# First modulation by single chunks of 128 channels, squares of x on PE, and groups of fours at other places of two projections and layer 1

## The chip, the cores and the metric

The kernel runs on one core of one Trainium2 chip. The metric is the time of one execution on the device, in microseconds; of several runs the median counts. The profile is that of one further execution, which the hardware profiler recorded.

## The reference

A latent stream x of 256 tokens and a context of 256 tokens, both of width 2048, go through two layers. Each layer first modulates the RMS norm of its input by shift and scale, which are products of a conditioning vector (SiLU of c, or of c_ctx for the context) with large matrices `ada_w`. Cut to what the change touches:

```
def _modulate(x, w, shift, scale):
    return _rmsnorm(x, w) * (1.0 + scale) + shift
...
sc, scc = silu(c), silu(c_ctx)
shift_x, scale_x, gate_x = split((sc @ ada_w[i] + ada_b[i])[:, None, :], 3)
shift_c, scale_c, gate_c = split(scc @ ada_w[i] + ada_b[i], 3)
hx = _modulate(x, norm_w[i], shift_x, scale_x)
hc = _modulate(ctx, norm_w[i], shift_c, scale_c)
...
# layer 0: p = hx @ w_in, cut into q, k, v, gates; retention and Fourier mixing; y @ w_out
# layer 1: bg, cg, xt, g = split(hx @ w_in, 4); y = bg * conv3(cg * xt) * silu(g); y @ w_out
x = x + gate_x * y
```

At the end stands a last RMS norm. All numbers are float32.

## The kernel before

**Numbers in two parts.** Float32 products are made on PE (TensorE) from two parts of each number. `whi` is a weight rounded to PE's fast 32-bit type (ACT casts, L94), `wlo` is the rest (DVE subtracts, L59). Activations are stored as 256 tokens of high part beside 256 of low part. A matmul with `whi` as the stationary operand streams all 512 columns, one with `wlo` only the 256 columns of the high part.

**Groups and pieces.** `group_t` makes 256 output channels. It loads 1 MB of weights at a time (`raw`), splits it into four pieces of 512 columns, and issues for each piece eight matmuls: four with `whi` (H0 to H3) and four with `wlo` (L0 to L3). Their order is a table: LOW alternates L0 H0 L1 H1, HIGH alternates H0 L0 H1 L1, FOURS has the four H and then the four L. An argument `orders` gives a pair, the table of a group's first piece and that of all others; default is LOW for both. SETTLE is (HIGH, FOURS), AFTER is (HIGH, LOW). `project` (first projection `w0o`, last projection `w1o`) uses groups of 16 pieces, b = 0 to 6: SETTLE in b = 1, AFTER in b = 2. Layer 1 (`w1`) has for each b = 0 to 15 four groups of 8 pieces, in the order tcg, txt, tbg, tg; SETTLE stands in tcg, AFTER in txt, for b = 1 and 2.

**The start.** x arrives in four tiles `xT`. `norm_sums` squares them on ACT, adds them on DVE (`nacc`) and sums over the 128 partitions by two matmuls with `ones`; root and reciprocal give `rs_x`. The modulation of 256 channels (one e of eight) needs 4 MB of `ada0`, in four loads (`load_ada`); `gemv` multiplies each with the conditioning (tile `gemv` in the profile), `gather` copies the sums (`gs`), `modulation` adds their four strips by four small products with `cols` and makes scale and shift (`md`), `mod_stream` writes the modulated x (`hx`) or context (`hc`). Then `main_k` and `main_v` multiply these 256 channels with 1 MB of `w0s`, into k, q and v of the first two heads (`pk`, `pq`, `pvx`; for the context `pk`, `pvc`). The loop over e does the main matmuls of e beside the gemv of e + 2.

**What sets the order.** Each engine runs its instructions in order. The order is made by a scheduler at build time, which moves instructions past each other as its own timeline sees fit; the source gives the priorities. Loads go out on the queue of SP, in order, and wait for a free buffer: three for `raw`, one each for the two others that `load_ada` uses (L237 to L248). `bg` and `hook` put other work between the pieces: the later modulation vectors (`adaT`, DVE) and, in layer 0, retention and Fourier steps. The Fourier products of the last channel groups (`pP`, `py`, `pz`) stand between the pieces of the first projection's b = 0 and 1.

Of the kernel before, what the change touches and what calls it, by code (L numbers as in the profile page):

```python
# [20 lines left out]
D = 2048  # L21
# [3 lines left out]
P = 128  # L25
# [10 lines left out]
def body(tc, a, out):  # L36
    nc = tc.nc
    es = ExitStack()
    with es:
# [88 lines left out]
        HIGH = "H0 L0 H1 L1 H2 L2 H3 L3".split()  # L128
        FOURS = "H0 H1 H2 H3 L0 L1 L2 L3".split()

        SETTLE, AFTER = (HIGH, FOURS), (HIGH, LOW)

        def group_t(wd, i0, nkt, streams, orders=(LOW, LOW)):

            ps = [psum("gT") for _ in streams]
            last = nkt * 8 - 1
            for kt in range(nkt):
                raw = load_raw(wd[i0 + kt])
                bg()
                for pc, (hi, lo) in enumerate(split_w(raw)):  # L140
                    todo = orders[kt + pc > 0]
                    seen = set()
                    for what, j in ((x[0], int(x[1])) for x in todo):
                        k2, m = j // 2, j % 2
                        kc, c0 = kt * 8 + pc * 2 + k2, j * 128
# [104 lines left out]
        def norm_sums(tiles, rs, ps):  # L250
            acc = rp.tile([P, 4, 256], F32, tag="m4", bufs=2, name="nacc")
            for q in range(4):
                if q == 0:
                    nc.scalar.square(acc[:], tiles[q][:])
# [7 lines left out]
            nc.scalar.activation(rs[:], ps[:, 0:256], AF.Sqrt, bias=eps[:], scale=1.0 / D)  # L262
            nc.vector.reciprocal(rs[:], rs[:])

        scol = const.tile([P, 32], F32, name="scol")
        nc.scalar.activation(scol[:], cols[:, C_C:C_C + 32], AF.Silu)
        nc.vector.tensor_copy(sc32[:, :, 0:16], scol[:, 0:16].unsqueeze(2).to_broadcast([P, 16, 16]))
# [6 lines left out]
        load_x(xT, a["xT"])  # L274
        
        pk, pvx, pvc = psum("pk"), psum("pvx"), psum("pvc")
        norm_sums(xT, rs_x, pvx[:, 0, :])
        gp, pq = bank("gemv"), bank("pq")

        def gemv(raw, kq):  # L280
# [29 lines left out]
        def main_k(e, k2, w):  # L310
            hi, lo = w
            kc = 2 * e + k2
            for x, blocks in ((hx[e], kq_x), (hc[e], k_c)):
# [7 lines left out]
        def main_v(e, k2, w):  # L321
            hi, lo = w
            kc = 2 * e + k2
            for x, t in ((hx[e], pvx), (hc[e], pvc)):
# [14 lines left out]
            return (rp.tile([P, 512], F32R, tag="sga", bufs=2, name="whi"),  # L339
                    rp.tile([P, 512], F32R, tag="ot", bufs=2, name="wlo"))  # L340

        mds = [prepare(0, load_ada(0))]
        mod_stream(0, mds[0], 0)
        wraw = load_raw(a["w0s"][0])
        load_x(cT, a["ctxT"])
        norm_sums(cT, rs_c, pvc[:, 0, :])
        mod_stream(0, mds[0], 1)
        mds.append(prepare(1, load_ada(1)))
        mod_stream(1, mds[1], 0)
        mod_stream(1, mds[1], 1)  # L350
        wn = split_w(wraw, spare)
        for e in range(8):
            w = wn
            more = e < 6
            if e < 7:
                wraw = load_raw(a["w0s"][e + 1])
            raws = load_ada(e + 2) if more else None
            main_k(e, 0, w[0])
            if more:
                gemv(raws[0], 0)  # L360
            main_v(e, 0, w[1])
# [5 lines left out]
            main_k(e, 1, w[2])  # L367
            if more:
                gemv(raws[3], 3)
                gs = gather()  # L370
            main_v(e, 1, w[3])
# [455 lines left out]
        def project(wd, xs, gcol, xin, acc, first=None, post=None):  # L827


            def res(b, m, v, src):  # L830
                nc.vector.scalar_tensor_tensor(x1[b][:, m, :], v, mods[:, gcol + 2 * b + m:gcol + 2 * b + m + 1],
                                               src[:, m, :], op0=ALU.mult, op1=ALU.add)

            tot = None
            for b in range(8):
                src = xin(b)
                quiet[0] = b >= 7 - (post is not None)
                if b < 7:
                    t = first if b == 0 and first is not None else group_t(wd, 4 * b, 4, [xs], *({1: (SETTLE,), 2: (AFTER,)}.get(b, ())))[0]
                    s = lr(l1, t)  # L840
                    for m in range(2):
                        res(b, m, s[:, m, :], src)
                    if b == 0:
                        nc.scalar.square(acc[:], x1[b][:])
                    else:
                        sq = l1.tile([P, 2, 256], F32, tag="t2", bufs=5, name="sq")
                        nc.scalar.square(sq[:], x1[b][:])
                        add(acc[:], acc[:], sq[:])
                    for m in range(2 if post is not None else 0):
                        nc.scalar.activation(x1[b][:, m, :], x1[b][:, m, :], AF.Copy,  # L850
                                             scale=cols[:, post + 2 * b + m:post + 2 * b + m + 1])
                else:
                    t = group_d(wd, 4 * b, 4, xs)
                    tot = bank("tot")
                    for m in range(2):
                        mm(tot[:, 0:256], ones[:], acc[:, m, :], m == 0, False)

                    warm = l1.tile([P, 1], F32, tag="warm", name="warm")
                    nc.scalar.activation(warm[:], acc[:, 0, 0:1], AF.Sqrt)
                    sq = l1.tile([P, 2, 256], F32, tag="t2", bufs=5, name="sq")  # L860
                    for m in range(2):
                        res(b, m, t[:, m * 256:m * 256 + 256], src)
                        nc.scalar.square(sq[:, m, :], x1[b][:, m, :])
                        mm(tot[:, 0:256], ones[:], sq[:, m, :], False, m == 1)
            return rstd_bc(l1, tot[:, 0:256], D)
# [17 lines left out]
        w1 = a["w1"]  # L883
        y1 = []
        for b in range(16):
            tcg, = group_t(w1, b * 8, 2, [h1], *((SETTLE,) if b in (1, 2) else ()))
            scg = lr(l1, tcg, "scg", 2)
            txt, = group_t(w1, b * 8 + 2, 2, [h1], *((AFTER,) if b in (1, 2) else ()))
            z = lr(l1, txt, "z", 2)
            mul(z[:], z[:], scg[:])  # L890
            cv = l1.tile([P, 2, 256], F32, tag="cv", bufs=2, name="cv")
            for m in range(2):
# [47 lines left out]
def _layout(i):  # L940
# [19 lines left out]
    a["ada0"] = s.reshape(32, P, 2048)  # L960
# [72 lines left out]
```

## Time and profile before

| | |
|---|---|
| runs of the kernel | 1822.88, 1823.37, 1826.58 us; median 1823.37 |
| the profiled execution | 1826.86 us |
| its span, first to last instruction | 1825.1 us |
| mean granted PE clock | 0.988 |
| busy share of the span | PE 97%, DVE 68%, ACT 49% |
| from HBM | 397.03 MB, 219 GB/s over the span |

The span runs from the first instruction to the last; the execution's own time has 1.8 us around it. A row of a timeline gives start, duration, engine, line, operation and operands, and in brackets how long the engine was idle before it and what released it. A matmul's duration is longer than the distance to the next matmul's start, since they overlap. A float32 product that isn't in two parts (gemv, ones, cols) has two records in the trace.

The stages, by the timeline: modulation and first heads to about 142 us, layer 0 with retention and Fourier to about 740, first projection to 916, layer 1 from 920 to about 1630, last projection to the end.

### The profile page before, as it was taken

How to read it: one execution, taken by the hardware profiler on the slowest of the kernel's cores; microseconds unless marked ns; L12 is line 12 of the kernel's file. 1: busy time of each engine (PE TensorE's matmuls, PEld its weight loads, DVE VectorE, ACT ScalarE, POOL GpSimd, SP SyncE). 2: the span in 40 equal slices, each digit the busy share in tenths (PEclk: the TensorE clock that was granted, in tenths of full speed). 3: DMA queues.
4: the chain of work that ended last, by engine and by line, in shares of the span. 5: the costliest groups of instructions: out<-in, count | busy, mean ns of one | idle time of the engine just before them, and what ended most of it. 6: DMA issues, size and time to landing. Idle time of an engine off the chain costs nothing.

```text
span 1825.1 us, 25950 instructions
## 1 busy us (share of the span) xinstructions
PE 1777.8 (97%) x10086; PEld 1514.6 (83%) x10086; DVE 1248.0 (68%) x2001; ACT 901.9 (49%) x1493; POOL 0.2 (0%) x4
## 2 busy tenths in 40 slices
PE   5999999999989999999999999999999999999997
PEld 3667888888877888888978888888888888888887
DVE  5348858758469788777677888666666666665554
ACT  4225626345455455444555555555555555555553
POOL 0000000000000000000000000000000000000000
PEclk9999999999989899999999999999999999999999
DMA  9886656655435556577647777555555555555552
GB/s 388 341 315 259 233 212 221 240 207 208 166 117 217 199 188 216 194 295 295 231 155 264 296 277 281 197 191 185 187 196 195 185 185 191 197 189 185 187 193 105
DMA packets 58732, 400.82 MB, mean 220 GB/s; under 512 B 6512, under 2 KB 6896, under 8 KB 11376
## 3 DMA queue, kind: packets, MB, share of 16 engines
q1 hardware_dynamic: 58608, 399.16, 59.8%
q8 instruction: 79, 1.29, 0.3%
q14 instruction: 45, 0.37, 0.1%
HBM read 397.03 MB, written 2.10 MB: 219 GB/s over the span
## 4 chain that ended last, share of the span: by engine, by line
PE 94%; DVE 3%; DMA 1%; ACT 1%; issue 0%; SPq 0%; DVEq 0%; ACTq 0%
PE gT L56 71%; PE gN L56 7%; PE gD L56 3%; PE pu L56 2%; PE gemv L56 2%; PE o L56 2%; PE pk L56 1%; PE pvx L56 1%; PE pvc L56 1%; PE pd L56 1%; DMA raw<-ada 1%; PE S L56 1%; PE pq L56 1%; DVE wlo L59 1%; PE pP L56 1%; PE py L56 0%
## 5 line engine op out<-in xcount | busy, mean ns | idle before, releaser
L94 ACT CAST whi<-raw 128x512 fp32r<-128x512 f32 x1024 | 628.3, 620 | 627.3 <-PE gT L56 469.4
L59 DVE TENSOR_TENSOR wlo<-raw,whi 128x512 fp32r<-128x512 f32 x1024 | 693.2, 688 | 344.4 <-ACT whi L94 334.5
L56 PE MATMUL gT<-h,whi 128*128 128x512 f32 x2048 | 707.6, 394 | 0.7 <-DVE h L215 0.7
L56 PE MATMUL gT<-h,wlo 128*128 128x256 f32 x2048 | 560.8, 278 | 3.4 <-ACT h L214 3.4
L56 PEld LDWEIGHTS gT<-h,whi 128*128 128x128 f32 x2048 | 383.3, 188 | 89.0 <-DVE h L215 1.2
L56 PEld LDWEIGHTS gT<-h,wlo 128*128 128x128 f32 x2048 | 383.4, 188 | 5.6 <-ACT h L214 3.8
L56 PE MATMUL gT<-hx,whi 128*128 128x512 f32 x576 | 209.4, 398 | 0.0
L388 DVE CUSTOM_DVE_ANT_0 raw<-raw,scb 128x2048 f32<-128x2048 f32 x64 | 146.5, 2290 | 54.0 <-DMA raw<-adaT 50.8
L56 PE MATMUL gT<-hx,wlo 128*128 128x256 f32 x576 | 165.2, 287 | 2.8 <-ACT v L507 1.6
L56 PE MATMUL gT<-y,whi 128*128 128x512 f32 x448 | 150.9, 394 | 0.0
L56 PEld LDWEIGHTS gT<-hx,whi 128*128 128x128 f32 x576 | 108.8, 189 | 21.3
L56 PEld LDWEIGHTS gT<-hx,wlo 128*128 128x128 f32 x576 | 109.5, 190 | 10.0 <-DVE wlo L59 2.7
L56 PE MATMUL gT<-y,wlo 128*128 128x256 f32 x448 | 116.9, 278 | 0.0
L56 PEld LDWEIGHTS gT<-y,whi 128*128 128x128 f32 x448 | 82.9, 188 | 18.2
L198 ACT COPY lr_r<-gT 128x512 f32<-128x512 f32 x103 | 60.5, 587 | 65.7 <-PE gT L56 65.4
L56 PEld LDWEIGHTS gT<-y,wlo 128*128 128x128 f32 x448 | 82.1, 188 | 1.4
L56 PE MATMUL gT<-yA,whi 128*128 128x512 f32 x224 | 77.5, 398 | 0.0
L56 PE MATMUL gT<-yB,whi 128*128 128x512 f32 x224 | 76.9, 398 | 0.0
L65 DVE TENSOR_TENSOR t<-gT,lr_r 128x512 f32<-128x512 f32 x68 | 46.9, 689 | 29.9 <-ACT lr_r L198 29.7
L56 PE MATMUL gT<-yA,wlo 128*128 128x256 f32 x224 | 59.9, 281 | 0.6 <-DVE wlo L59 0.6
L56 PE MATMUL gN<-whi,hx 128*128 128x512 f32 x192 | 59.7, 392 | 0.0
L56 PE MATMUL gN<-whi,hc 128*128 128x512 f32 x192 | 59.7, 391 | 0.0
(283 smaller groups left out, 2162.0 us busy)
## 6 DMA issues: line engine op xcount, KB each, us to landing
raw<-w SPq DMA_DIRECT2D x168, 1024.0 KB, 4.8
raw<-adaT SPq DMA_DIRECT2D x64, 1024.0 KB, 4.9
raw<-ada SPq DMA_DIRECT2D x32, 1024.0 KB, 7.1
raw<-w0o SPq DMA_DIRECT2D x32, 1024.0 KB, 4.8
raw<-w1o SPq DMA_DIRECT2D x32, 1024.0 KB, 4.8
raw<-w0g SPq DMA_DIRECT2D x16, 1024.0 KB, 4.8
raw<-w0u SPq DMA_DIRECT2D x16, 1024.0 KB, 4.9
raw<-w0s SPq DMA_DIRECT2D x8, 1024.0 KB, 5.6
```

The source lines that it names most:

```text
L56: nc.tensor.matmul(o, l, r, start=start, stop=stop, skip_group_check=True)
L59: nc.vector.tensor_tensor(o, x, hi.bitcast(F32), op=ALU.subtract)
L65: nc.vector.tensor_tensor(o, x, y, op=ALU.add)
L94: nc.scalar.copy(hi, x)
L198: nc.scalar.copy(r[:], t[:, :, 256:512])
L388: nc.vector.tensor_tensor_reduce(out=raw[:], in0=raw[:], in1=scb[:], scale=1.0, scalar=0.0, op0=ALU.mult, op1=ALU.add, accum_out=gv[:, j:j ...
```

## The change

1. **Start.** The first 256 channels (e = 0) are modulated in two chunks of 128. The first four loads of `ada0` are laid out anew on the host, so that two loads hold all that one chunk needs. `load_first`, `first` and `mod_first` do load, gemv and modulation of one chunk; the main matmuls of x for a chunk follow it at once, those of the context stay in the loop (argument `only`). The loads of the second chunk go into other buffers than raw.
2. **Squares of x.** `norm_sums_pe` squares half a tile on ACT and sums it by two matmuls with ones, 16 in all; DVE adds nothing. The context keeps `norm_sums`.
3. **Fours.** SETTLE and AFTER are now lists of eight orders, one for each piece; `group_t` steps through the list it is given and begins again at its end. In `project`, b = 3 and b = 4 have SETTLE + AFTER (first half, second half of a group); b = 1 and 2 are LOW. In layer 1, tcg and txt keep theirs in b = 1 and 2, and tbg and tg get SETTLE and AFTER in b = 0 and 1, so that the two alternate from b = 0's third group to b = 2's second.

```diff
-        SETTLE, AFTER = (HIGH, FOURS), (HIGH, LOW)
+        SETTLE, AFTER = [HIGH] + [FOURS] * 7, [HIGH] + [LOW] * 7
...
-                    todo = orders[kt + pc > 0]
+                    todo = orders[(kt * 4 + pc) % len(orders)]
...
+        def norm_sums_pe(tiles, rs, ps):
+            for q in range(4):
+                for h in range(2):
+                    sq = rp.tile([P, 2, 256], F32, tag="t2", bufs=5, name="sq2")
+                    nc.scalar.square(sq[:], tiles[q][:, 2 * h:2 * h + 2, :])
+                    for k in range(2):
+                        i = 4 * q + 2 * h + k
+                        mm(ps[:, 0:256], ones[:], sq[:, k, :], i == 0, i == 15)
...
-        mds = [prepare(0, load_ada(0))]
-        mod_stream(0, mds[0], 0)
+        r0 = load_first(0)
         wraw = load_raw(a["w0s"][0])
+        r1 = load_first(1)
+        m0 = first(0, r0)
+        mod_first(0, m0, 0)
+        wn = split_w(wraw, spare)
         load_x(cT, a["ctxT"])
+        main_k(0, 0, wn[0], (0,))
+        main_v(0, 0, wn[1], (0,))
+        m1 = first(1, r1)
+        mod_first(1, m1, 0)
+        main_k(0, 1, wn[2], (0,))
+        main_v(0, 1, wn[3], (0,))
+        raws1 = load_ada(1)
         norm_sums(cT, rs_c, pvc[:, 0, :])
-        mod_stream(0, mds[0], 1)
-        mds.append(prepare(1, load_ada(1)))
+        mod_first(0, m0, 1)
+        mod_first(1, m1, 1)
+        mds = [None, prepare(1, raws1)]
...
-            main_k(e, 0, w[0])
+            streams = (0, 1) if e else (1,)
+            main_k(e, 0, w[0], streams)
...
-                    t = first if b == 0 and first is not None else group_t(wd, 4 * b, 4, [xs], *({1: (SETTLE,), 2: (AFTER,)}.get(b, ())))[0]
+                    t = first if b == 0 and first is not None else group_t(wd, 4 * b, 4, [xs], SETTLE + AFTER if b in (3, 4) else (LOW,))[0]
...
-            tcg, = group_t(w1, b * 8, 2, [h1], *((SETTLE,) if b in (1, 2) else ()))
+            tcg, = group_t(w1, b * 8, 2, [h1], SETTLE if b in (1, 2) else (LOW,))
...
-            tbg, = group_t(w1, b * 8 + 4, 2, [h1])
+            tbg, = group_t(w1, b * 8 + 4, 2, [h1], SETTLE if b in (0, 1) else (LOW,))
...
-            tg, = group_t(w1, b * 8 + 6, 2, [h1])
+            tg, = group_t(w1, b * 8 + 6, 2, [h1], AFTER if b in (0, 1) else (LOW,))
```

The new functions of the first chunk:

```
def first(k2, raws):
    for i in range(2):
        for j in range(8):
            t = j % 4
            mm(gp[32 * t:32 * t + 32, 0:256], sc32[:, i * 8 + j, :], raws[i][:, j * 256:j * 256 + 256],
               i == 0 and j < 4, i == 1 and j > 3)
    gs = rp.tile([P, 512], F32, tag="cst", name="gs")
    nc.vector.tensor_copy(gs[:, 0:256], gp[:, 0:256])
    for n in range(2):
        mm(gp[:, 2 * n:2 * n + 2], gs[:, n * 128:n * 128 + 128], cols[:, C_SEL:C_SEL + 2], True, True)
    ...
    return md
def mod_first(k2, md, s):
    dst, src, rs = ((hx, xT, rs_x), (hc, cT, rs_c))[s]
    modulate(rp, dst[0][:, k2, :], src[0][:, k2, :], md[:, 0, s:s + 1], md[:, 1, s:s + 1], rs)
```

**The order of the loads on SP.** Before, the queue at the start stands so (ada is a quarter of one e, xT and cT the tiles of x and of the context):

```order
L85 DMA raw<-ada 128x2048
L244 DMA raw<-ada 128x2048
L85 DMA raw<-ada 128x2048
L244 DMA raw<-ada 128x2048
L85 DMA raw<-w0s 128x2048
L235 DMA cT_103<-ctxT 128x1024
L235 DMA cT_104<-ctxT 128x1024
L235 DMA cT_105<-ctxT 128x1024
L235 DMA cT_106<-ctxT 128x1024
```

Now, on the same queue behind the same four tiles of x:

```order
L85 DMA raw<-ada 128x2048 x2
L85 DMA raw<-w0s 128x2048
L361 DMA raw<-ada 128x2048 x2
L235 DMA cT_103<-ctxT 128x1024
L235 DMA cT_104<-ctxT 128x1024
L235 DMA cT_105<-ctxT 128x1024
L235 DMA cT_106<-ctxT 128x1024
L85 DMA raw<-ada 128x2048 x2
L85 DMA raw<-w0s 128x2048
L244 DMA raw<-ada 128x2048 x2
```

The first w0s stands ahead of the second pair of ada. Of the four loads of e = 1, which came one after the other ahead of the second w0s, two come behind it now.

**PE around the second gemv.** Before, on PE, where the gemv of e = 1 and the first context matmuls meet (hx_80 and hc_88 are x and context of e = 0):

```order
L56 MATMUL gemv<-raw,sc_79 32x512 x8
L56 MATMUL pvc<-nacc,ones 128x256 x2
L56 MATMUL pk<-hx_80,whi 128x256 x2
L56 MATMUL pk<-hx_80,wlo 128x256
L56 MATMUL pk<-hx_80,whi 128x256 x2
L56 MATMUL pk<-hx_80,wlo 128x256
L56 MATMUL gemv<-raw,sc_79 32x512 x4
L56 MATMUL pk<-hc_88,whi 128x256
L56 MATMUL pvc<-whi,hc_88 128x512
L56 MATMUL gemv<-raw,sc_79 32x512 x4
```

Now, at the same place:

```order
L56 MATMUL pvx<-wlo,hx_80 128x512
L56 MATMUL pvc<-nacc,ones 128x256 x2
L56 MATMUL gemv<-raw,sc_79 32x512 x12
L56 MATMUL pk<-hc_88,whi 128x256
L56 MATMUL pvc<-whi,hc_88 128x512
L56 MATMUL pk<-hc_88,whi 128x256
L56 MATMUL pk<-hc_88,wlo 128x256
```

The matmuls of x for e = 0 are all ahead of this place; three quarters of the gemv stand in one piece ahead of all context matmuls. On ACT and DVE the cast and split of the second w0s has moved ahead of the root and the reciprocal of `rs_c`.

**PE in the first projection.** Before, part of b = 1 (py and pz are Fourier products):

```order
L56 MATMUL gT<-yA_2404,whi 128x512 x4
L56 MATMUL gT<-yA_2404,wlo 128x256 x2
L56 MATMUL py<-ph,zh 128x256
L56 MATMUL py<-ph,zl 128x256
L56 MATMUL gT<-yA_2404,wlo 128x256 x2
L56 MATMUL py<-pl,zh 128x256
```

Now, where b = 3 begins:

```order
L56 MATMUL gT<-yA_1550,whi 128x512
L56 MATMUL gT<-yA_1550,wlo 128x256
L56 MATMUL gT<-yA_1554,whi 128x512 x4
L56 MATMUL gT<-yA_1554,wlo 128x256 x4
L56 MATMUL gT<-yA_2444,whi 128x512 x4
L56 MATMUL gT<-yA_2444,wlo 128x256 x4
L56 MATMUL gT<-yA_2448,whi 128x512 x4
```

The fours stood among Fourier products and stand now among matmuls of the projection alone.

More of the change, by code (lines that the diff above doesn't have):

```diff
@@ L129, in body, with group_t @@
         FOURS = "H0 H1 H2 H3 L0 L1 L2 L3".split()
-        SETTLE, AFTER = (HIGH, FOURS), (HIGH, LOW)
-        def group_t(wd, i0, nkt, streams, orders=(LOW, LOW)):
+        SETTLE, AFTER = [HIGH] + [FOURS] * 7, [HIGH] + [LOW] * 7
+        def group_t(wd, i0, nkt, streams, orders=(LOW,)):
             ps = [psum("gT") for _ in streams]
@@ L263, in norm_sums @@
             nc.vector.reciprocal(rs[:], rs[:])
+        def norm_sums_pe(tiles, rs, ps):
[6 more added lines that the diff above has]
+                        mm(ps[:, 0:256], ones[:], sq[:, k, :], i == 0, i == 15)
+            nc.scalar.activation(rs[:], ps[:, 0:256], AF.Sqrt, bias=eps[:], scale=1.0 / D)
+            nc.vector.reciprocal(rs[:], rs[:])
         scol = const.tile([P, 32], F32, name="scol")
@@ L276, in body @@
         pk, pvx, pvc = psum("pk"), psum("pvx"), psum("pvc")
-        norm_sums(xT, rs_x, pvx[:, 0, :])
+        norm_sums_pe(xT, rs_x, pvx[:, 0, :])
         gp, pq = bank("gemv"), bank("pq")
@@ L308, in mod_stream, with main_k @@
                          md[:, 2 + k2, s:s + 1], rs)
-        def main_k(e, k2, w):
+        def main_k(e, k2, w, only=(0, 1)):
             hi, lo = w
             kc = 2 * e + k2
-            for x, blocks in ((hx[e], kq_x), (hc[e], k_c)):
+            for x, blocks in [((hx[e], kq_x), (hc[e], k_c))[i] for i in only]:
                 xh, xl = x[:, k2, 0:256], x[:, k2, 256:512]
@@ L319, in main_k, with main_v @@
                     mm(o, lo[:, c0:c0 + 128], xh, False, kc == 15)
-        def main_v(e, k2, w):
+        def main_v(e, k2, w, only=(0, 1)):
             hi, lo = w
             kc = 2 * e + k2
-            for x, t in ((hx[e], pvx), (hc[e], pvc)):
+            for x, t in [((hx[e], pvx), (hc[e], pvc))[i] for i in only]:
                 for m in range(2):
@@ L340, in spare, with load_first @@
                     rp.tile([P, 512], F32R, tag="ot", bufs=2, name="wlo"))
-        mds = [prepare(0, load_ada(0))]
-        mod_stream(0, mds[0], 0)
+        def load_first(k2):
+            got = []
+            for i in range(2):
+                if k2:
+                    raw = (rp.tile([P, 2048], F32, tag="v", bufs=1, name="raw") if i == 0
+                           else wp.tile([P, 2048], F32, tag="scb", bufs=1, name="raw"))
+                    nc.sync.dma_start(raw[:], a["ada0"][2 * k2 + i])
+                else:
+                    raw = load_raw(a["ada0"][2 * k2 + i])
+                got.append(raw)
+            return got
@@ new lines, in first @@
+        def first(k2, raws):
+            for i in range(2):
+                for j in range(8):
+                    t = j % 4
+                    mm(gp[32 * t:32 * t + 32, 0:256], sc32[:, i * 8 + j, :], raws[i][:, j * 256:j * 256 + 256],
+                       i == 0 and j < 4, i == 1 and j > 3)
+            gs = rp.tile([P, 512], F32, tag="cst", name="gs")
+            nc.vector.tensor_copy(gs[:, 0:256], gp[:, 0:256])
+            for n in range(2):
+                mm(gp[:, 2 * n:2 * n + 2], gs[:, n * 128:n * 128 + 128], cols[:, C_SEL:C_SEL + 2], True, True)
+            md = rp.tile([P, 4, 2], F32, tag="md", bufs=2, name="md")
+            for n in range(2):
+                c = C_AB0 + 16 * n + k2
+                add(md[:, n, :], gp[:, 2 * n:2 * n + 2], cols[:, c:c + 1].to_broadcast([P, 2]))
+            mul(md[:, 0, :], md[:, 0, :], cols[:, C_NW0 + k2:C_NW0 + k2 + 1].to_broadcast([P, 2]))
+            return md
@@ L344, in body @@
+        def mod_first(k2, md, s):
+            dst, src, rs = ((hx, xT, rs_x), (hc, cT, rs_c))[s]
+            modulate(rp, dst[0][:, k2, :], src[0][:, k2, :], md[:, 0, s:s + 1], md[:, 1, s:s + 1], rs)
+        r0 = load_first(0)
         wraw = load_raw(a["w0s"][0])
+        r1 = load_first(1)
+        m0 = first(0, r0)
+        mod_first(0, m0, 0)
+        wn = split_w(wraw, spare)
         load_x(cT, a["ctxT"])
+        main_k(0, 0, wn[0], (0,))
+        main_v(0, 0, wn[1], (0,))
+        m1 = first(1, r1)
@@ L346, in body @@
+        mod_first(1, m1, 0)
+        main_k(0, 1, wn[2], (0,))
+        main_v(0, 1, wn[3], (0,))
+        raws1 = load_ada(1)
         norm_sums(cT, rs_c, pvc[:, 0, :])
-        mod_stream(0, mds[0], 1)
-        mds.append(prepare(1, load_ada(1)))
+        mod_first(0, m0, 1)
+        mod_first(1, m1, 1)
+        mds = [None, prepare(1, raws1)]
         mod_stream(1, mds[1], 0)
         mod_stream(1, mds[1], 1)
-        wn = split_w(wraw, spare)
         for e in range(8):
@@ L357, in body @@
             raws = load_ada(e + 2) if more else None
-            main_k(e, 0, w[0])
+            streams = (0, 1) if e else (1,)
+            main_k(e, 0, w[0], streams)
             if more:
                 gemv(raws[0], 0)
-            main_v(e, 0, w[1])
+            main_v(e, 0, w[1], streams)
             if e < 7:
@@ L366, in body @@
                 gemv(raws[2], 2)
-            main_k(e, 1, w[2])
+            main_k(e, 1, w[2], streams)
             if more:
@@ L370, in body @@
                 gs = gather()
-            main_v(e, 1, w[3])
+            main_v(e, 1, w[3], streams)
             if more:
@@ L885, in body @@
         for b in range(16):
-            tcg, = group_t(w1, b * 8, 2, [h1], *((SETTLE,) if b in (1, 2) else ()))
+            tcg, = group_t(w1, b * 8, 2, [h1], SETTLE if b in (1, 2) else (LOW,))
             scg = lr(l1, tcg, "scg", 2)
-            txt, = group_t(w1, b * 8 + 2, 2, [h1], *((AFTER,) if b in (1, 2) else ()))
+            txt, = group_t(w1, b * 8 + 2, 2, [h1], AFTER if b in (1, 2) else (LOW,))
             z = lr(l1, txt, "z", 2)
@@ L959, in _layout @@
     s = s.reshape(2, 4, 4, P, 8, 256).transpose(4, 1, 3, 2, 0, 5)
-    a["ada0"] = s.reshape(32, P, 2048)
+    s = s.reshape(32, P, 2048)
+    f0 = np.stack([ada[0][:, D:D + 256], ada[0][:, 0:256]]).reshape(2, 2, 8, P, 2, P)
+    s[0:4] = f0.transpose(4, 1, 3, 2, 0, 5).reshape(4, P, 2048)
+    a["ada0"] = s
     g = np.concatenate([ada[0][:, 2 * D:].T, ada[1][:, D:2 * D].T, ada[1][:, 0:D].T, ada[1][:, 2 * D:].T])
```

## Prediction

> **What bounds the kernel now.** I read the page first, then windows of the first microseconds, the timeline of PE, DVE and ACT up to 50 us, and last the starts of single matmuls, since the change is mostly one of order on PE.
>
> ```profile
> PE 94%; DVE 3%; DMA 1%; ACT 1%; issue 0%; SPq 0%; DVEq 0%; ACTq 0%
> ```
> PE carries 94% of the chain that ended last. So time can come from two places alone: the start, where PE idles, and the pace of back-to-back matmuls. Both are touched.
>
> ```profile
> 0.00:20.00 20.00, 6.16 (x28) 1.93 (x28) 7.07 (x12) 8.99 (x10) 0.20 (x4) 1.00 0.90 349
> 20.00:40.00 20.00, 14.22 (x78) 8.83 (x74) 12.04 (x20) 7.63 (x12) 0.00 (x0) 0.83 1.02 419
> 40.00:60.00 20.00, 19.60 (x131) 13.54 (x131) 8.58 (x20) 6.92 (x14) 0.00 (x0) 1.00 0.91 367
> ```
> The second number of a row is PE's busy time, the last ones are the granted clock, the DMA share and GB/s. In the first 40 us PE idles for 19.6 us while the DMAs are full (419 GB/s in the second row). From 40 us on PE is full and the DMAs are not. So the start waits for data, not for PE.
>
> **The start, step by step.** When do loads land?
>
> ```profile
> 13.36 1.94 PE L56 MATMUL gemv<-raw,sc 128*32 128x512 f32 x8 [13.36 <-DMA raw<-ada]
> 20.72 1.07 PE L56 MATMUL gemv<-raw,sc 128*32 128x512 f32 x8 [0.50 <-DMA raw<-ada]
> 23.20 2.17 ACT L94 CAST whi<-raw 128x512 fp32r<-128x512 f32 x4 [4.84 <-DMA raw<-w0s]
> 25.84 0.58 PE L56 MATMUL pq<-hx,whi 128*128 128x256 f32 x1 [2.19 <-ACT hx L214]
> 41.82 2.18 ACT L94 CAST whi<-raw 128x512 fp32r<-128x512 f32 x4 [1.07 <-DMA raw<-w0s]
> ```
> The first and the fourth 1 MB load of ada land at 13.36 and 20.72: three loads in 7.36 us, 2.45 us per MB. The next, w0s, lands at 23.20, again 2.48 us later. The queue is thus a line of loads at about 2.47 us each, and the new SP order says when each lands: ada 13.4 and 15.8, w0s 18.3, the second pair of ada 20.7 and 23.2, ctxT (2 MB) by 28.2, then two quarters of the next ada at 30.7 and 33.2, **the second w0s at 35.7**, and the other two quarters at 38.1 and **40.6**. Before, all four quarters came ahead of that w0s (41.82), so the last of them by about 38.3: it moves back by some 2.4 us.
>
> ```profile
> 5.06 1.06 ACT L254 ACTIVATE nacc<-xT 128x1024 f32<-128x1024 f32 x1 [0.30 <-DMA xT<-xT]
> 15.78 2.08 PE L56 MATMUL pvx<-nacc,ones 128*128 128x256 f32 x4 [0.48 <-DVE nacc L65]
> 35.85 1.13 PE L56 MATMUL pvc<-nacc,ones 128*128 128x256 f32 x4
> 37.53 1.75 DVE L263 RECIPROCAL rs_c<-rs_c 128x256 f32<-128x256 f32 x1 [2.76 <-ACT rs_c L262]
> 40.40 0.39 PE L56 MATMUL pk<-hc,whi 128*128 128x256 f32 x1 [1.71 <-ACT hc L214]
> 40.95 1.06 PE L56 MATMUL gemv<-raw,sc 128*32 128x512 f32 x8
> 41.94 0.38 PE L56 MATMUL pk<-hc,whi 128*128 128x256 f32 x1
> 43.80 0.40 PE L56 MATMUL pk<-hx,whi 128*128 128x256 f32 x2
> 45.94 0.95 PE L56 MATMUL gemv<-cols,gs 128*128 128x2 f32 x8
> 48.62 0.39 PE L56 MATMUL pk<-hx,whi 128*128 128x256 f32 x1
> ```
> Squares of x on PE: 16 matmuls with ones in place of 2. Two cost 2.08 us at 15.78 and 1.13 us at 35.85, so 16 take 9 to 17 us. They start after the first half square (x is there at 5.06), at about 5.7, and run where PE idled; they end near 17.5, as the two did before (15.78 + 2.08 = 17.86). rs_x therefore comes no earlier. If they ran cold to the end (5.7 + 16.6 = 22.3) the first modulation would lose what it gains, and nothing later.
>
> First chunk: its two loads are there at 15.8, so its gemv follows the squares, near 17.5 to 19.7, and rs_x (0.47 us on ACT, 1.75 on DVE, both behind the squares) at 20.3. From the old end of gemv (20.72 + 1.07 = 21.79) to the first main matmul (25.84) were 4.05 us; without the wait, with half the copy, some 2.6 remain: **first main matmul near 22.9, 2.9 us earlier**.
>
> Is that kept? Not if the second round (e = 1) starts as before. It needs the last quarter of ada. The new PE order puts the gemv of quarters two to four in one piece ahead of the context's matmuls, and the sums that gather the modulation (cols) behind them. So: last quarter lands at 40.6, gemv 1.06, 41.7. Beside it the context's path: the second w0s is cast and split on ACT and DVE ahead of rs_c now (35.7 + 2.2 on ACT, lo done by 39.1), then the reciprocal 1.75 (40.9), then 1.12 to the first context matmul as before (37.53 + 1.75 = 39.28 to 40.40): 42.0. The context's matmuls: 10 of a chunk's 12 took 43.80 - 41.94 = 1.86, so 2.2 per chunk, 4.4 for both: 46.4. The four cols products 0.95: 47.4. From there to the first matmul of e = 1 were 48.62 - 46.89 = 1.73: **49.1 against 48.62, +0.5 us**. The early work was done while PE would have waited anyway. From there PE is full (19.6 of 20 us), so these 0.5 us run through to the end. Bounds: -2.9 (all of the earlier start kept) and +2.9:
>
> ```profile
> 22.30:25.70 3.40, 1.05 (x8) 0.97 (x8) 2.22 (x8) 2.50 (x6) 0.00 (x0) 1.00 1.03 412
> 25.70:32.50 6.80, 5.69 (x18) 4.60 (x19) 4.87 (x7) 4.22 (x6) 0.00 (x0) 0.50 1.02 424
> ```
> After 3.4 us with 1.05 us of PE work the clock was at half for 6.8 us. The changed order has a thin stretch too, about 29 to 33 us, ahead of the second chunk (its modulation stands behind the context's squares on ACT and DVE). At half clock the chunk's 2.5 us, the two sums and the gemv behind it end 2 to 2.5 us later.
>
> The page "TensorE: Matmul & The Clock Gate" of the Trainium skill, Part 1, says that an idle window of about 3.4 us halves the clock and that such windows run freely; the rows agree in size, so whether this stretch is caught may differ between executions.
>
> **The pace, step by step.** Now the order in groups. Whi matmuls have 512 columns, wlo matmuls 256.
>
> ```profile
> 779.00:879.00 100.00, 100.00 (x568) 1.00 0.79 295
> 980.00:1010.00 30.00, 30.00 (x175) 1.00 0.82 289
> 1027.00:1127.00 100.00, 100.00 (x579) 1.00 0.76 284
> 1680.00:1780.00 100.00, 100.00 (x579) 1.00 0.53 188
> ```
> These windows, of PE's work on gT alone, hold nothing but alternating wlo and whi, at full clock, PE never idle. Each lies right behind a group of fours: that of the first projection, the two of layer 1, that of the last projection. Yet the first holds 568 in 100 us and the last two 579 (the second, shorter, 175 in 30): a piece of eight takes 1.408 or 1.382 us. **There are two paces, 0.027 us a piece apart,** and each holds until something breaks the alternation. A piece of fours:
>
> ```profile
> 776.59 1.09 PE L56 MATMUL gT<-yB,whi 128*128 128x512 f32 x4
> ...
> 777.99 0.40 PE L56 MATMUL gT<-yA,whi 128*128 128x512 f32 x1
> ```
> From its first whi to the next piece's are 1.40 us: between the two paces. So fours cost 0.02 a piece where the pace is fast, gain at most 0.01 where it is slow, and their worth is the pace they leave behind. Here, behind 777.99, the slow pace was in force.
>
> Terms: layer 1. Fours now stand in the third group already; if they leave the fast pace, one group of 8 at 0.027 comes earlier (-0.2), fours in slow pace -0.07, and one more group of fours in fast pace costs +0.15: **-0.1 us**. First projection: the fours of b = 1 were cut by Fourier products; 7 and 7 in b = 3 and b = 4 stand free. If they settle, half of b = 3 and b = 4 and all of b = 5 and 6 gain, 16 + 32 pieces by 0.027 = -1.3; if not, nothing (fours in a slow stretch, -0.1, against the lost ones of b = 1, +0.1). Bounds -1.4 and +0.1; I take 0, since the same order before left it slow. The last projection has its fours moved likewise, inside a fast stretch: 0.
>
> **Sum:** +0.5 - 0.1 + 0 = **+0.4 us** on the profiled 1826.86. That execution was 3.5 us over the median of the runs (1823.37), so on the median: 1823.7.
>
> **The rivals.**
> Layer 1 does not settle (slower). Before, its first fours followed two pieces in high-first order; now one piece. A slow stretch repeats every three pairs, so where in it the fours begin is another place. One group of fours of the first projection shows what may happen:
>
> ```profile
> 746.99 1.07 PE L56 MATMUL gT<-yA,whi 128*128 128x512 f32 x4
> ...
> 748.49 0.40 PE L56 MATMUL gT<-yB,whi 128*128 128x512 f32 x1
> 748.72 0.28 PE L56 MATMUL gT<-yB,wlo 128*128 128x256 f32 x1
> 748.84 0.40 PE L56 MATMUL gT<-yB,whi 128*128 128x512 f32 x1
> 749.08 0.28 PE L56 MATMUL gT<-yB,wlo 128*128 128x256 f32 x1
> 749.20 0.40 PE L56 MATMUL gT<-yB,whi 128*128 128x512 f32 x1
> ```
> Its four whi took 1.07 where those at 776.59 took 1.09, and the pairs behind it are of 0.35 and 0.36, the slow pace. If the new first fours are of that kind, they leave the slow pace in force as at 777.99, and since each block (one piece high-first, seven of fours, one high-first, seven low-first) repeats the one before it, every try may fail alike. Price: layer 1's 512 pieces less 24 before and 28 fours, and 96 of the last projection's: some 556 by 0.027 = +15.0, 1826.86 + 15.4, on the median 1838.8. Against it: three of the four groups of fours left the fast pace (the windows at 980, 1027 and 1680). It decides from one matmul's place in the cycle.
>
> The earlier start is kept (faster): if the context's path does not wait for the second w0s, e = 1 starts 2.9 earlier; with the projection settled -2.9 - 1.3 - 0.1 = -4.3, on the median 1819.1. For it: PE idles there; against it: the loads' line, which carries the same bytes.
>
> Order does nothing. The same page of the skill, "Back-to-back issue gap", has a spacing set by the columns of a matmul and its weight load. As a mechanism here: fours change no pace, the fast pace of layer 1 comes from something else and stays, and +0.5 is left, 1823.9. The rows of 568 and 579, equal in columns, speak against it.
>
> **How the numbers follow.** A measurement tells about 0.2%, 3.65 us, from no change. Forecast 0.48, and its own range 1821 to 1827 takes the projection's -1.4 and the half clock's +2.5; layer 1 unsettled 0.32; start kept 0.15; order does nothing 0.05. Faster (under 1819.7) 0.15 + 0.01 = 0.16; slower (over 1827.0) 0.32 + 0.01 = 0.33; same 0.51. The range must reach both rivals: 1818.5 to 1840.5.
>
> **What would show it.** The first main matmul near 23 and that of e = 1 near 49 (start); windows of 100 us in layer 1 with 579 matmuls (settled) or 568 (not), the same in the projection behind b = 4; PE's granted clock between 29 and 40 us. The forecast is wrong if e = 1 starts before 46 us, or if any long stretch of layer 1 shows 0.353 a pair.

## The result, and the profile after

| | before | after |
|---|---|---|
| median of the runs, us | 1823.12 (1822.84 to 1826.58) | 1835.71 (1835.28 to 1837.79) |
| ratio to before | | 1.0067, 95% interval 1.0049 to 1.0084 |
| the profiled execution's span, us | 1825.1 | 1833.7 |

The change costs 12.6 us. The forecast was +0.4; its first rival, layer 1 that does not settle, was priced at +15.4. The range of 1818.5 to 1840.5 holds 1835.71 because it was drawn to reach that rival, not because the forecast had the mechanism. The chain of waits of the changed kernel names the same bound as before, with a little more PE:

```profile
PE 95%; DVE 2%; DMA 1%; ACT 1%; SPq 0%; issue 0%; DVEq 0%; ACTq 0%
```

The windows of PE's work on gT, at the same times as those of before (the count in brackets, then the granted clock):

```profile
779.00:879.00 100.00, 100.00 (x569) 1.00 0.78 290
1027.00:1127.00 100.00, 100.00 (x568) 1.00 0.74 277
1680.00:1780.00 100.00, 100.00 (x570) 1.00 0.53 187
```

Where before had 568, 579 and 579 there are now 569, 568 and 570. PE is never idle and its clock is full in all of them, so the matmuls themselves come at the slower pace, through all of layer 1 and the last projection.

Where the spans part is read from the first gT matmul of each stage: layer 0 (hx), layer 1 (h) and last projection (y). The timeline of PE before:

```profile
157.38 0.39 PE L56 MATMUL gT<-hx,wlo 128*128 128x256 f32 x1 [1.64 <-ACT v L507]
919.81 0.44 PE L56 MATMUL gT<-h,wlo 128*128 128x256 f32 x1 [3.41 <-ACT h L214]
1633.40 0.27 PE L56 MATMUL gT<-y,wlo 128*128 128x256 f32 x1
```

and after:

```profile
154.62 0.39 PE L56 MATMUL gT<-hx,wlo 128*128 128x256 f32 x1 [0.79 <-ACT v L564]
913.73 0.45 PE L56 MATMUL gT<-h,wlo 128*128 128x256 f32 x1 [3.41 <-ACT h L214]
1639.46 0.28 PE L56 MATMUL gT<-y,wlo 128*128 128x256 f32 x1
```

| stage | before, us | after, us | difference |
|---|---|---|---|
| start and first heads (to gT on hx) | 157.38 | 154.62 | -2.8 |
| layer 0 and first projection (to gT on h) | 762.43 | 759.11 | -3.3 |
| layer 1 (to gT on y) | 713.59 | 725.73 | +12.1 |
| last projection to the end of the span | 191.7 | 194.2 | +2.5 |

The third and fourth row together are 14.6 us, the rival's loss. Of the first row a part belongs to the two executions and not to the change (see the section on the start). The second is mostly not the change's: that stage took between 758.0 and 762.0 us in the profiles of the kernels below that have the slower pace in the first projection, whichever start they have (fours_alone, with the start of before, 758.1; no_fours, with the new one, 761.8). The profiled execution of before was also 3.5 us over its median. So the 8.6 us between the two spans understate the loss.

At the start the windows show PE filled where it idled (before: 6.16 and 14.22 us busy):

```profile
0.00:20.00 20.00, 11.46 (x68) 8.58 (x68) 5.04 (x15) 11.22 (x18) 0.20 (x4) 0.99 0.90 358
20.00:40.00 20.00, 15.55 (x100) 9.29 (x100) 11.23 (x19) 7.91 (x12) 0.00 (x0) 0.84 1.02 419
```

The timeline of PE after, with the steps that the prediction dated:

```profile
5.90 8.87 PE L56 MATMUL pvx<-sq,ones 128*128 128x256 f32 x32 [5.90 <-ACT sq L270]
...
20.78 0.58 PE L56 MATMUL pk<-hx,whi 128*128 128x256 f32 x1 [2.77 <-ACT hx L214]
...
40.64 1.06 PE L56 MATMUL gemv<-raw,sc 128*32 128x512 f32 x8 [0.56 <-DMA raw<-ada]
...
48.52 0.39 PE L56 MATMUL pk<-hx,whi 128*128 128x256 f32 x1
```

The first main matmul is 5.1 us earlier than before (25.84), that of e = 1 only 0.1 us (48.62). Other profiles say the same: the first product with cols of e = 1 came at 45.31 to 46.59 us in the three that have the start of before (before, before_eight, fours_alone), and at 45.50 to 47.25 in those that have the new one.

**How a piece of fours shows its kind.** The timeline groups the four wlo of each piece of fours in one row. In the first try of the changed kernel (layer 1, b = 0):

```profile
941.19 0.64 PE L56 MATMUL gT<-h,wlo 128*128 128x256 f32 x4
941.67 1.09 PE L56 MATMUL gT<-h,whi 128*128 128x512 f32 x4
942.60 0.63 PE L56 MATMUL gT<-h,wlo 128*128 128x256 f32 x4
...
949.61 0.64 PE L56 MATMUL gT<-h,wlo 128*128 128x256 f32 x4
```

These rows go 0.64, 0.63, 0.64 and so on: two kinds of pieces in turn, seven in all, the last of 0.64. The unrounded starts show the kinds too: from the first wlo to the next piece's first whi it is 477 or 478 ns in the one and 471 in the other. In the kernel before, the first try of layer 1 (b = 1):

```profile
969.85 0.63 PE L56 MATMUL gT<-h,wlo 128*128 128x256 f32 x4
...
978.27 0.63 PE L56 MATMUL gT<-h,wlo 128*128 128x256 f32 x4
```

Seven as well, but from 0.63 to 0.63. Behind it the faster pace holds, behind the other the slower one. The experiments test three things: that the kind of the **last** piece decides, that the kinds alternate, and that the first one is set by where in the three-pair cycle of the slower pace the group is entered.

### The profile page after: what moved, and what is told of

Read it like the earlier page. It is cut to its first block, busy times and chain, and to the rows that moved or that the text cites. A ratio compares the mean times of both kernels' runs of the same rounds, so it can differ in the third digit from the quotient of the medians.

```text
span 1833.7 us, 26100 instructions
## 1 busy us (share of the span) xinstructions
PE 1795.7 (98%) x10146; PEld 1527.0 (83%) x10146; DVE 1242.1 (68%) x2001; ACT 899.3 (49%) x1496; POOL 0.2 (0%) x4
## 4 chain that ended last, share of the span: by engine, by line
PE 95%; DVE 2%; DMA 1%; ACT 1%; SPq 0%; issue 0%; DVEq 0%; ACTq 0%
PE gT L56 72%; PE gN L56 7%; PE gD L56 3%; PE pu L56 2%; PE gemv L56 2%; PE o L56 2%; PE pk L56 1%; PE pvx L56 1%; PE pvc L56 1%; PE pd L56 1%; PE S L56 1%; DMA raw<-w0s 1%; PE pP L56 1%; PE pq L56 1%; DMA raw<-ada 1%; PE py L56 1%
## 5 line engine op out<-in xcount | busy, mean ns | idle before, releaser
L56 PE MATMUL gT<-h,whi 128*128 128x512 f32 x2048 | 715.3, 399 | 0.7 <-DVE h L215 0.7
L56 PE MATMUL gT<-yB,wlo 128*128 128x256 f32 x224 | 62.4, 281 | 0.0
```

Source lines behind the costliest of these rows:

```text
L56: nc.tensor.matmul(o, l, r, start=start, stop=stop, skip_group_check=True)
```

## The experiments

Each line compares with runs of the kernel before on the same chip; seven_two_later has two runs, the others four to ten. The two counts are the gT matmuls in the windows 1027 to 1127 (layer 1) and 1680 to 1780 (last projection).

| run | median, us | ratio to before, 95% interval | layer 1 | last projection |
|---|---|---|---|---|
| head_alone | 1835.40 | 1.0057, 1.0044 to 1.0070 | 567 | 569 |
| fours_alone | 1837.46 | 1.0068, 1.0054 to 1.0083 | 568 | 569 |
| eight_fours | 1820.57 | 0.9979, 0.9970 to 0.9988 | 579 | 577 |
| two_fours | 1820.43 | 0.9978, 0.9968 to 0.9988 | 579 | 577 |
| before_eight | 1837.83 | 1.0066, 1.0053 to 1.0080 | 568 | 580 |
| head_eight | 1820.62 | 0.9981, 0.9972 to 0.9990 | 579 | 578 |
| seven_later | 1820.90 | 0.9976, 0.9966 to 0.9986 | 579 | 577 |
| seven_two_later | 1836.54 | 1.0064, 1.0046 to 1.0083 | 568 | 569 |
| no_fours | 1837.38 | 1.0072, 1.0048 to 1.0096 | 569 | 568 |
| squares_alone | 1823.22 | 0.9994, 0.9985 to 1.0003 | 579 | 579 |
| chunk_two | 1820.11 | 0.9975, 0.9966 to 0.9984 | 579 | 577 |
| best_two_places | 1818.60 | 0.9969, 0.9958 to 0.9981 | 579 | 579 |

### One half of the change at a time

fours_alone is the kernel before with all lines on `orders` of the diff. head_alone is the changed kernel with the fours of before:

```
-  ... group_t(wd, 4 * b, 4, [xs], SETTLE + AFTER if b in (3, 4) else (LOW,))[0]
+  ... group_t(wd, 4 * b, 4, [xs], [HIGH] + [FOURS] * 15 if b == 1 else [HIGH] + [LOW] * 15 if b == 2 else (LOW,))[0]
-  tbg, = group_t(w1, b * 8 + 4, 2, [h1], SETTLE if b in (0, 1) else (LOW,))
+  tbg, = group_t(w1, b * 8 + 4, 2, [h1])
-  tg, = group_t(w1, b * 8 + 6, 2, [h1], AFTER if b in (0, 1) else (LOW,))
+  tg, = group_t(w1, b * 8 + 6, 2, [h1])
```

> The changed start (single chunks, squares on PE) with the groups of fours where they stood before. Theory A (what the changed kernel lost, it lost by the new places of the fours; the start gained 2.7 us by the end of the first heads): layer 1 and the last projection at 579 gT matmuls per 100 us as before, first gT of layer 0 near 154.6 us, time 2.7 us under the kernel before, about 1820.4. Theory B (the shifted start itself puts layer 1 in the slower pace): 570 per 100 us in layer 1 and about 1835. Theory C (the start brings nothing of its own, the first 6 us of lead came by clock windows): about 1823.

> The start of before with the fours at their new places. Theory A: layer 1 at 570 gT matmuls per 100 us, 14.7 us over the kernel before less up to 0.6 gained in the first projection, about 1837.5. Theory B (the start does it): 579 per 100 us in layer 1 and about 1823.

The new fours lose it by themselves (13.0 us), as theory A has it. But so does the new start (11.0 us), with the fours where they were: A fell for head_alone, C (1823) with it, and B's number came. The built order shows how a change in the first 150 us reaches layer 1 at 950. Its first two groups are interleaved by the scheduler, and their matmuls 84 to 109, counted from 0 (H with whi, L with wlo, and the number of the h tile), stand so, before and in head_alone:

```
before      H3 H6 L6 H6 L7 H7 L7 H7 L7 L4 H4 L4 H4 L4 H4 L4 H4 H7 L7 H7 L5 H5 L5 H5 L5 H5
head_alone  H3 H6 L6 H6 L7 H7 L7 H7 L7 L4 H4 L4 H4 L4 H4 H7 L7 H7 L4 H4 L5 H5 L5 H5 L5 H5
```

The last place where two whi stand side by side (H4 H7 in both) comes one pair earlier in head_alone, and in the two groups together the alternation is broken eight times where before had ten. From there to the fours both have the same order, but the three-pair cycle is entered elsewhere: the last whi ahead of the high-first matmuls (two pieces of them in both) is the one of 232 ns before and the one of 241 ns in head_alone (intervals between starts, worked out from the traces). The first piece of fours is then of the other kind:

```profile
962.79 0.64 PE L56 MATMUL gT<-h,wlo 128*128 128x256 f32 x4
...
971.21 0.64 PE L56 MATMUL gT<-h,wlo 128*128 128x256 f32 x4
```

The first and the last of the seven are of 0.64 where before had 0.63, and the window of layer 1 holds 567. Whether something else of the start, data or clock, holds layer 1 back is what head_eight tests.

### The number of fours

eight_fours keeps one try of the changed kernel, and two_fours one with two pieces; later tries are gone in both:

```
# eight_fours
tbg, = group_t(w1, b * 8 + 4, 2, [h1], SETTLE if b == 0 else (LOW,))
tg, = group_t(w1, b * 8 + 6, 2, [h1], [FOURS, HIGH] + [LOW] * 6 if b == 0 else (LOW,))
# two_fours
tbg, = group_t(w1, b * 8 + 4, 2, [h1], [HIGH, FOURS, FOURS, HIGH] + [LOW] * 4 if b == 0 else (LOW,))
```

> The changed kernel, but layer 1 has fours in one place only, b = 0: one piece high-first, eight of fours (not seven), one high-first, and low-first from there on. Theory A1 (pieces of fours come in two kinds that alternate; the group starts with the kind that leaves the slower pace in force, so an odd number ends in it and an even number ends in the other kind): layer 1 at 579 per 100 us behind the group, no second try needed, last projection fast too, 14.5 to 15 us under the changed kernel, about 1821. Theory A2 (fours at this early place don't settle, whatever their number): 570 per 100 us and about 1836.

> The changed kernel, but layer 1 has only two pieces of fours in all, b = 0 in tbg: one piece high-first, two of fours, one high-first, then low-first. Theory A1 (the number being even decides): 579 per 100 us behind the group, about 1821. Theory A3 (a longer stretch of fours is needed to settle): 570 per 100 us, about 1836.

Both came out at 1820.5. Two pieces do what seven could not. The timeline of two_fours:

```profile
941.06 0.64 PE L56 MATMUL gT<-h,wlo 128*128 128x256 f32 x4
941.54 1.09 PE L56 MATMUL gT<-h,whi 128*128 128x512 f32 x4
942.47 0.63 PE L56 MATMUL gT<-h,wlo 128*128 128x256 f32 x4
```

The same first kind as in the changed kernel, one of the other kind behind it, and the faster pace from there on (579).

An even number is not good in itself. before_eight takes the kernel before and makes its first try one piece longer; head_eight does the same to head_alone (in both: tcg of b = 1 as SETTLE, txt of b = 1 as below, no later try):

```
txt, = group_t(w1, b * 8 + 2, 2, [h1], [FOURS, HIGH] + [LOW] * 6 if b == 1 else (LOW,))
```

> The kernel before with one try in layer 1 (b = 1, where its first one stood), of eight pieces of fours in place of seven. Theory A1 (the kind of the first piece is set by where in the three-pair cycle the group is entered, then the kinds alternate): here the first is of the kind that an odd number needs, so eight end in the slower pace: 569 gT matmuls per 100 us in layer 1 and in the last projection, about 14.5 us over the kernel before, 1838.5. Theory A4 (an even number is good anywhere): 579 and about 1824.

> The changed start with the fours of before, but in layer 1 one try at b = 1, of eight pieces in place of seven. Theory A1 (the changed start moved the point in the cycle at which the fours of layer 1 are entered, so its first piece is of the other kind): eight settle, 579 per 100 us, about 1821 against 1835.4 with seven. Theory B1 (something else of the start, data or clock, keeps layer 1 slow): 569 and about 1835.5.

One piece more costs the kernel before 13 us and gains 15 in head_alone. The first and the eighth piece of before_eight in the timeline:

```profile
967.75 0.63 PE L56 MATMUL gT<-h,wlo 128*128 128x256 f32 x4
...
977.57 0.64 PE L56 MATMUL gT<-h,wlo 128*128 128x256 f32 x4
```

A1's forecast for before_eight missed in one place: its last projection has 580, since the fours of its own b = 1 found the faster pace there. head_eight also settles B1: under the same new start one piece more brings the faster pace, so neither its data nor its clock holds layer 1 back. That the moved pair is what shifted the entry is read from the orders and not tested by itself: the traces show ten breaks in the four kernels without the single chunks and eight in the ten with them.

### The place where they are entered

seven_later is the changed kernel with one try of seven, begun one piece later; seven_two_later begins it two pieces later:

```
# seven_later
tbg: [LOW, HIGH] + [FOURS] * 6        tg: [FOURS, HIGH] + [LOW] * 6
# seven_two_later
tbg: [LOW, LOW, HIGH] + [FOURS] * 5   tg: [FOURS, FOURS, HIGH] + [LOW] * 5
```

> The changed kernel with one try in layer 1 of seven pieces of fours, as it has it at b = 0, but begun one piece later (one more low-first piece ahead). Theory A1: four pairs later is the next place of the three-pair cycle (the last whi ahead of the high-first piece at 236 ns instead of 241), from which the first piece of fours is of the other kind; so seven settle here: 579 gT matmuls per 100 us in layer 1, about 1821. Rival A5 (in the changed kernel an odd number fails wherever it stands): 569 and about 1836.

> The same, begun two pieces later than in the changed kernel. Theory A1: the last whi ahead of the high-first piece is at 233 ns, from which the changed kernel's second try failed; so seven fail again: 569 in layer 1, about 1836. Rival A6 (any place but the changed kernel's own will do): 579 and about 1821.

One piece of delay gains 15 us, two gain nothing. A piece is four pairs, so the three kernels (the changed one and these two) enter at the three places of the three-pair cycle: the last whi ahead of the high-first piece is of 241, 235 and 233 ns, and the first piece of fours is of the 0.64, the 0.63 and again the 0.64 kind. The first and last pieces of seven_two_later are of 0.64 again, those of seven_later of 0.63 (timeline):

```profile
943.37 0.63 PE L56 MATMUL gT<-h,wlo 128*128 128x256 f32 x4
...
951.79 0.63 PE L56 MATMUL gT<-h,wlo 128*128 128x256 f32 x4
```

The place tells the kind only for the same number of matmuls in between. The kernel before has nearly the same last whi as seven_two_later (232 and 233 ns), but two high-first pieces behind it where the other has one, and its first piece is of the other kind.

no_fours takes every fours and high-first piece out of the changed kernel (`orders` is (LOW,) everywhere).

> The changed kernel with no piece of fours and none high-first anywhere: low-first in both projections and in layer 1. Theory A1 (the changed kernel's fours settle nothing, so they bring only their own piece's 0.01 us against the slower pace): 569 in layer 1 and last projection, within 1 us of the changed kernel, 1835 to 1837. Rival A7 (the fours themselves cost time, and low-first alone would find the faster pace): 579 and about 1820.

With 1.0072 against the changed kernel's 1.0067 the two can't be told apart: 56 pieces of fours bought nothing.

### The start

squares_alone is the kernel before with one line changed; chunk_two is two_fours with that line undone:

```
-  norm_sums(xT, rs_x, pvx[:, 0, :])
+  norm_sums_pe(xT, rs_x, pvx[:, 0, :])
```

> The kernel before with only the squares of x on PE (16 products with ones). First main matmul at 25.8 as before, since it waits for the fourth quarter of ada, not for the squares (theory S1); at 23.5 or earlier if the sums were what it waited for (S2). In the built order each later round has three runs of gemv among the main matmuls in place of four: if each such run costs PE 0.45 us on its own (theory G), the first gT of layer 0 is 2.0 to 2.7 us earlier than before though the first main matmul isn't; if runs cost nothing, within 0.5 of before. Layer 1 may be in either pace, as its entry may move: 1821 or 1836.

> two_fours with the sums of squares of x as before (ACT and DVE, two products with ones) and the single chunks kept. Theory H1 (what the start gained is the order of gemv in the later rounds, which is the same here, and not the early first matmul): first main matmul later than 20 us by up to 2, but e = 1 at 48 to 49 and the first gT of layer 0 within 0.5 us of two_fours (154.3); 1820.4 to 1821. Theory H2 (the squares on PE matter): layer 0 and the end 1 to 2 us later, 1821.5 to 1822.5.

In squares_alone the first main matmul came at 26.47 us (before 25.84), and yet the first gT of layer 0 at 155.49 (before 157.38):

```profile
26.47 0.58 PE L56 MATMUL pq<-hx,whi 128*128 128x256 f32 x1 [4.07 <-ACT hx L214]
...
155.49 0.39 PE L56 MATMUL gT<-hx,wlo 128*128 128x256 f32 x1 [1.63 <-ACT v L519]
```

That is 1.9 us, just short of theory G's 2.0 to 2.7, and this time alone proves nothing: before_eight, whose start is that of before, has its first gT at 155.22. The rounds below are the better measure. Nor can the runs of squares_alone be told from before (0.9985 to 1.0003). Its layer 1 has the order of before and kept 579. In chunk_two the first main matmul comes 3 us later than in two_fours (19.88; H1 had said up to 2), and the first gT at the same time (two_fours 154.28):

```profile
22.90 0.58 PE L56 MATMUL pk<-hx,whi 128*128 128x256 f32 x1 [0.40 <-ACT hx L214]
...
154.39 0.38 PE L56 MATMUL gT<-hx,wlo 128*128 128x256 f32 x1 [0.79 <-ACT v L564]
```

The medians agree too (1820.11 and 1820.43), though the granted clock from 20 to 40 us was 0.83 in the profile of two_fours and 1.00 in that of chunk_two. So the earlier first matmul is worth nothing (H1), and the gain lies behind the start of e = 1. One round of before begins so (timeline of PE):

```profile
63.38 1.07 PE L56 MATMUL gemv<-raw,sc 128*32 128x512 f32 x8 [0.32 <-DVE md L65]
64.57 0.39 PE L56 MATMUL pk<-hx,whi 128*128 128x256 f32 x1
...
65.23 1.06 PE L56 MATMUL gemv<-raw,sc 128*32 128x512 f32 x8
66.23 0.39 PE L56 MATMUL pk<-hx,whi 128*128 128x256 f32 x1
...
79.34 1.07 PE L56 MATMUL gemv<-raw,sc 128*32 128x512 f32 x8 [0.32 <-DVE md L65]
```

and the same round after:

```profile
63.14 1.92 PE L56 MATMUL gemv<-raw,sc 128*32 128x512 f32 x16 [0.32 <-DVE md L65]
65.00 0.39 PE L56 MATMUL pk<-hx,whi 128*128 128x256 f32 x1
...
78.60 1.92 PE L56 MATMUL gemv<-raw,sc 128*32 128x512 f32 x16 [0.32 <-DVE md L65]
```

Two runs of gemv took 1.19 and 1.00 us to the next matmul, one run of the same work takes 1.86. The round as a whole has shrunk from 15.96 to 15.46 us. Before, the first four of the six rounds had four runs of gemv each and the last two had three; after, all six have three. The times of the first product with cols, of e = 1 and of e = 7, enclose the six rounds (timeline of PE; the wait is the idle time in the row of the first gT):

| profile | cols of e = 1 | cols of e = 7 | six rounds | first gT of layer 0 | from cols of e = 7 to it | granted clock there | wait |
|---|---|---|---|---|---|---|---|
| before | 45.94 | 140.90 | 94.96 | 157.38 | 16.48 | 0.90 | 1.64 |
| before_eight (start of before) | 45.31 | 140.29 | 94.98 | 155.22 | 14.93 | 1.00 | 1.63 |
| squares_alone | 46.03 | 139.32 | 93.29 | 155.49 | 16.17 | 0.89 | 1.63 |
| after | 46.06 | 139.63 | 93.57 | 154.62 | 14.99 | 0.89 | 0.79 |
| eight_fours (start of after) | 47.25 | 140.80 | 93.55 | 154.85 | 14.05 | 1.00 | 1.28 |

The six rounds gained 1.4 us. The first four gained 1.8, and the last two, which had three runs before as well, lost 0.4; why is open. In squares_alone, where three rounds went from four runs to three, the gain is 1.7. Theory G's 0.45 a run fits the first (4 by 0.45 = 1.8) and roughly the second (3 by 0.45 = 1.35). The stretch behind the rounds gained 1.5 us at the lower clock and 0.9 at the full one; a shorter wait ahead of the first gT is part of it, with the chunks and not with the squares. How much the clock moves that gT is shown by the same code in two executions, before and before_eight:

```profile
140.90:157.38 16.48, 12.79 (x70) 10.86 (x68) 13.32 (x26) 11.59 (x16) 0.00 (x0) 0.90 0.66 259
140.29:155.22 14.93, 11.25 (x69) 9.57 (x67) 11.85 (x25) 11.46 (x16) 0.00 (x0) 1.00 0.61 234
```

So the 2.8 us are a figure of two executions: the first gT came at 155.22 to 157.38 in the three profiles with the start of before, and at 154.13 to 155.68 in the ten with the single chunks. Joining the runs of gemv and changing nothing else was not tried.

The start's whole worth is head_eight against before, which differ by it and by one try less, both at the faster pace: 0.9981, 3.5 us, with an interval from 1.8 to 5.1.

### Both halves put right

best_two_places is two_fours with the same short group in the first projection, and no fours in the last:

```
-  ... SETTLE + AFTER if b in (3, 4) else (LOW,) ...
+  ... [HIGH, FOURS, FOURS, HIGH] + [LOW] * 12 if b == 3 and first is not None else (LOW,) ...
```

> The changed kernel with two pieces of fours in all at two places: layer 1, b = 0, as in two_fours, and first projection, b = 3, in the same form (one high-first, two fours, one high-first, low-first); none in the last projection. Theory A1 (the changed kernel enters b = 3 with the same kind of piece first as layer 1): the first projection at 579 per 100 us behind b = 3, 60 pieces by 0.027 less, 1.6 us under two_fours, and 0.2 from the last projection: 1818.6. If b = 3 is not settled by two: 1820.2.

It came out at 1818.60, and the windows of the first projection, behind the fours at 796 us, and of the last show the faster pace (the changed kernel has 569 per 100 us in the first projection):

```profile
790.00:840.00 50.00, 50.00 (x290) 1.00 0.82 304
1680.00:1780.00 100.00, 100.00 (x579) 1.00 0.54 190
```

It beats the kernel before by 5.7 us (0.9969, 0.9958 to 0.9981). The step over two_fours, 1.8 us by the medians, is within what the intervals can't tell; its windows show it.

## Point by point

**What bounds.** Right: the chain gives PE 95%, the loss is the pace of the matmuls on PE, and the gain is mostly their order there.

**First main matmul, "near 22.9".** It came at 20.78. The 16 squares cost 8.87 us, at the lower end of the 9 to 17, so they ended at 14.77 and not at 17.5, and the first modulation moved with them. chunk_two, without them, has 22.90.

**"49.1 against 48.62, +0.5 us".** 48.52; the loads stood as forecast (last quarter, gemv at 40.64). The early work was done while PE would have waited.

**"These 0.5 us run through to the end".** Failed. PE was full from there, but not with a fixed amount of work: the scheduler joined runs of gemv in the later rounds. The term was -2.8 in place of +0.5 between these two profiles; 1.4 of it lies in the rounds and 1.5 in the stretch behind them (0.9 at full clock). The gain has the size of the rival "the earlier start is kept" (-2.9) but not its cause, as chunk_two shows. The prediction took the order of PE only up to e = 1 into account.

**Half clock, up to +2.9.** The stretch can be caught, but costs less. The changed kernel's profile had the full clock from 29 to 34 us. Of the kernels with the new start, head_alone and two_fours had 0.66 there, seven_later 0.69, seven_two_later 0.64 and eight_fours 0.86. Their first product with cols of e = 1 came at 45.50, 45.57, 47.21, 46.73 and 47.25 us, against 45.67 to 46.06 in those at full clock: up to 1.6 us later and not 2 to 2.5, in two of the five not later at all.

**"Layer 1 ... -0.1 us".** The step that decided, and it failed. The prediction had the first fours bring the faster pace; they kept the slower one, as the sign that it named (0.353 a pair over a long stretch) shows. The term was +12.1, with +2.5 for the last projection, whose 0 rested on its lying "inside a fast stretch". I gave the settling more weight because "three of the four groups of fours left the fast pace". That counted outcomes whose entries were not alike. The rival had the mechanism ("one matmul's place in the cycle"), the reason why the second try fails like the first, and the size: 15.0 us against 14.6. What it lacked was the alternation of two kinds of pieces. It also told the kinds by the wrong rows, four whi of 1.07 or 1.09 us: both of its examples, at 746.99 and 776.59, were followed by the slower pace, and in the changed kernel's try at 940 the whi of both kinds have 1.09. With the alternation, seven pieces must end in the kind in which they begin, and whether the first try settles hangs on its first piece alone: no count of earlier groups could weigh that.

**First projection, 0 with bounds -1.4 and +0.1.** Right in the number: 569 per 100 us against 568. The reason given, "the same order before left it slow", names no cause: before, Fourier products broke the fours up, now they stand whole, and by the traces both end in the 0.64 kind. Its fours are entered with the first kind too, so seven and seven failed; two were enough in best_two_places.

**"Order does nothing".** Fell: kernels that differ in the order of a few matmuls hold 567 to 569 of them in the window of layer 1 or 579, and none anything between. From whi to whi a pair takes 346.7 ns in the faster pace and 353.3 in the slower (means from 1300 to 1400 us, before and after). The Trainium skill, page "TensorE: Matmul & The Clock Gate", "Back-to-back issue gap", gives single spacings of 518 and 262 cycles at 2.4 GHz for 512 and 256 columns; a pair would take 325 ns by that (an estimate), in any order. The trace differs: it has two spacings, both longer, and the measurement decides.

## What to carry to other kernels

When a stream of alternating matmuls has two paces, find what leaves each of them, piece by piece, before moving or counting anything: here one piece of fours more or fewer was worth 13 to 15 us, and a try that works is no evidence for the same try at another place. A change at the start can reach such a state some 800 microseconds later through the scheduler's order alone, so the windows of every later stage belong to the check of a change. And where PE is full, count its runs of different kinds of matmul, not only its matmuls.

## What was not expected of the hardware

- The two paces last long, and across the border between stages: in two_fours pairs of 346.7 ns from the fours at 942 us to those of the last projection at 1694, through groups whose inputs and weights differ, at full clock (1.00 in both windows).
- Pieces of four whi and four wlo come in two kinds that differ by 2 to 9 ns (635 to 641 and 632 or 633 for the four wlo) and strictly alternate, in all 66 unbroken groups of fours in the traces, of two to fifteen pieces. Where alternating pieces follow (61 groups), the pace behind went with the kind of the last piece each time. Why, inside PE, stays open.
- A run of float32 products (gemv) between products in two parts has a price of its own: 2.19 us for two runs of eight records, 1.86 for one of sixteen, so 0.33 for one run more. Rounds with four runs took 15.95 to 16.17 us and rounds with three 15.43 to 15.82, in before, after and squares_alone.
